# Two feed-forward entries: planned powers on GpSimd, another home for the samples' rows, smaller result tiles

## The chip, the cores and the metric

One core of a Trainium2 chip runs the whole program. The metric is the device time of one execution in microseconds (us); less is better. The engines are named as in the profile: PE (TensorE matmuls; PEld its weight loads), DVE (VectorE), ACT (ScalarE), POOL (GpSimd) and SP (SyncE, which issues all the DMAs of this kernel).

## The reference

The program is one step of a two-layer decoder trunk, for 1024 prompt tokens and 64 sample tokens (8 sequences of 8), width 1024, all in float32. Layer 0 mixes tokens with a gated MLP (gMLP), layer 1 with sliding-window attention. After either mixer comes the same pair of norms and then a SwiGLU feed-forward part. The change sits around the second and third line of this loop body:

```python
out = mixer(rms_norm(x))                    # gMLP @ sg_w_out, or attention @ sw_w_o + sw_b_o
x = x + rms_norm(out, norm_post[layer])
h = rms_norm(x, f_norm_pre[layer])
x = x + rms_norm((silu(h @ w_gate) * (h @ w_up)) @ w_down, f_norm_post[layer])
```

where `rms_norm(x, g) = x * rsqrt(mean(x*x) + 1e-6) * g`.

## The kernel before

Every float32 operand of a matmul is held as a high and a low half, and a product is three matmuls. The high half is an ACT copy, the low half a DVE subtraction.

The kernel runs through these stages: gMLP mixer, its projection (`project`), the entry into the first feed-forward part, the two feed-forward products, the exit, then keys, values, queries and attention, the second projection with a bias, the second entry and the second feed-forward part. The tokens are nine blocks: blocks 0 to 7 are 128 prompt rows each, block 8 (`NB`) the 64 sample rows. In the projection's second half the blocks come in the order 0 to 6, 8, 7.

**The entry** is what this case is about. For each block, PE runs a chain of 24 matmuls (block 8: 16) into a PSUM bank. Then ACT squares it with a row sum (L1005), DVE multiplies by the norm's weight (L1009), DVE makes the mean (L938) and POOL raises it to a power (L939), DVE adds the scaled result to the residual rows in two instructions (L1014) and SP stores them (L1015). ACT squares the sum (L1036), DVE and POOL make mean and power again (L938, L939; the samples' rows are 64 high), and ACT makes the normalised copy h (L1039). The residual rows come by DMA (L995) into a ring of 3 tiles named `rows`.

The feed-forward product uses a scheme with fewer products: seven operand forms, x1, x2 and y2, taken from the h blocks directly, and t1 to t4, differences of them (DVE, L1081, 128x512 each). The form t2 of pair i needs h of the blocks i and i+4, so the last ones need blocks 7 and 3. Each form is turned by PE transposes into one of three PSUM banks `aux` (L1051; the samples' turn is L1101), and each bank is then copied to a high half by ACT (L1055) and a low half by DVE (L1059). PE multiplies by the weights meanwhile (`part`, L1271 to L1273). Weights of the feed-forward part arrive by DMA in `raw` tiles (L416), ACT scales them (L424, four instructions) and makes the high half (L1611, or L340 elsewhere), DVE the low half (L1615, L341) and the sums of two weights (L360 to L363).

**What sets the order.** For PE, ACT and DVE in the entry, `Plan` writes the order when the program is built. It is a list scheduler: each task has an engine, a cost from the table `TIME`, the tasks it waits for, and resources that it takes and gives back (`act` and `tmp` tiles, the `rows` ring, PSUM banks `bank` and `aux`). Mean and power are one task on DVE, with the power's time as a delay behind it. The order on each engine is then kept as written: an instruction whose input is late holds up all that stand behind it. Elsewhere a scheduler of the compiler sets the order, from due times that the kernel gives it.

**Tiles of the mixers' results.** `rows` of the projection are 16 `act` tiles in the class whose methods are `at` and `pieces`: one tile for each of 8 features and each half of 512 tokens. They are given back eight at a time, behind the chains of blocks 3 and 7.

**The bias rows** of the second projection (`ones2`, `ones8` and `both`) are made at the head of `project`: POOL memsets and casts (L1137 to L1144), a DMA of `in_sw_b_o`, and a split. Each chain of the second projection ends in one matmul with them (L1154).

## Time and profile before

| what | us |
|---|---|
| median of 3 runs | 2172.33 (2169.41 to 2173.25) |
| the profiled execution, its own time | 2174.07 |
| its span, first to last instruction | 2172.3 |
| PE busy | 2122.9 (98%) |
| DVE, ACT, POOL busy | 1360.2 (63%), 1041.2 (48%), 191.0 (9%) |

The profile is of one execution. The entry of layer 0 lies at about 303 to 376 us, the attention stage at about 1083 to 1345 us, the second projection from 1345 us and the second entry's end at about 1475 us. Beside busy time the trace gives the clock that TensorE was granted: 1.00 is 2.4 GHz, 0.50 is 1.2 GHz.

### The profile page before, as it was taken

Reading aid. Unit: us, or ns where it says so; the run is one execution under the profiler, and the core shown is the slowest. Engines: PE = TensorE matmul, PEld = TensorE weight load, DVE = VectorE, ACT = ScalarE, POOL = GpSimd, SP = SyncE. Lnnn points to the kernel's source line nnn. Section 1 sums busy time; section 2 is a strip of 40 time slices with the busy share of each in tenths; the row PEclk is TensorE's granted clock in tenths of the full one; section 3 lists DMA queues with packets and bytes.
Section 4 is the critical chain, followed back from the end, with each engine's and each line's share of the span. In section 5 each row is a group of like instructions: output and inputs, shape, how many; then the busy total and the mean of one; then the engine's idle time right before and its main releaser. Section 6 shows DMA issues by size and latency. Waiting matters only on the chain.

```text
span 2172.3 us, 29400 instructions
## 1 busy us (share of the span) xinstructions
PE 2122.9 (98%) x11088; PEld 1817.3 (84%) x11088; DVE 1360.2 (63%) x2147; ACT 1041.2 (48%) x2083; POOL 191.0 (9%) x226
## 2 busy tenths in 40 slices
PE   8999998999999999999899999999999999999998
PEld 7999987788888888888698887878888888888886
DVE  5455557656665666566757767467656666665676
ACT  5234555444444443434657655365444454434342
POOL 1322301000000000000402222020000000000001
PEclk9999999999999999999899998999999999999999
DMA  4210332232232328756432111241232232268574
GB/s 146 67 39 30 97 111 93 69 99 90 94 101 87 105 97 300 243 189 215 154 87 52 48 35 55 79 145 55 95 98 95 100 97 79 95 229 289 174 255 148
DMA packets 175492, 257.11 MB, mean 118 GB/s; under 512 B 24515, under 2 KB 104629, under 8 KB 175350
## 3 DMA queue, kind: packets, MB, share of 16 engines
q1 hardware_dynamic: 175350, 255.24, 36.0%
q8 instruction: 87, 1.43, 0.3%
q14 instruction: 55, 0.45, 0.1%
HBM read 188.96 MB, written 60.62 MB: 115 GB/s over the span
## 4 chain that ended last, share of the span: by engine, by line
PE 90%; DVE 5%; DMA 2%; ACT 2%; issue 1%; POOL 1%; SPq 0%; POOLq 0%; DVEq 0%; ACTq 0%
PE bank L1497 14%; PE bank L1271 12%; PE bank L1272 12%; PE bank L1273 12%; PE bank L580 5%; PE bank L581 5%; PE bank L582 4%; PE aux L1497 4%; PE bank L957 2%; PE bank L958 2%; PE bank L959 2%; PE bank L1351 2%; PE bank L1350 2%; PE aux L1505 2%; PE aux L1051 1%; PE aux L878 1%
## 5 line engine op out<-in xcount | busy, mean ns | idle before, releaser
L1271 PE MATMUL bank<-act,act 128*128 128x512 f32 x1232 | 486.5, 395 | 4.1 <-DVE tmp L1405 4.1
L1272 PE MATMUL bank<-act,act 128*128 128x512 f32 x1232 | 483.9, 393 | 2.3 <-DVE act L1059 2.3
L1273 PE MATMUL bank<-act,act 128*128 128x512 f32 x1232 | 481.0, 391 | 0.0
L1497 PE MATMUL bank<-act,act 128*128 128x512 f32 x1452 | 341.7, 389 | 0.0
L341 DVE TENSOR_TENSOR act<-raw,act 128x1024 fp32r<-128x1024 f32 x201 | 245.6, 1223 | 126.6 <-ACT act L340 118.8
L1497 PEld LDWEIGHTS bank<-act,act 128*128 128x128 f32 x1452 | 272.4, 188 | 56.5
L340 ACT ACTIVATE act<-raw 128x1024 fp32r<-128x1024 f32 x201 | 212.4, 1059 | 214.8 <-PE bank L1351 73.7
L1271 PEld LDWEIGHTS bank<-act,act 128*128 128x128 f32 x1232 | 232.7, 189 | 50.3 <-DVE tmp L1405 5.0
L1273 PEld LDWEIGHTS bank<-act,act 128*128 128x128 f32 x1232 | 232.3, 189 | 49.4
L1272 PEld LDWEIGHTS bank<-act,act 128*128 128x128 f32 x1232 | 232.7, 189 | 46.3 <-DVE act L1059 2.8
L586 ACT ACTIVATE act<-act 128x1024 fp32r<-128x1024 f32 (+5 forms) x194 | 166.0, 904 | 186.7 <-PE bank L1497 66.7
L587 DVE TENSOR_TENSOR act<-act,act 128x1024 fp32r<-128x1024 f32 (+5 forms) x194 | 194.2, 1042 | 57.0 <-ACT act L586 43.3
L580 PE MATMUL bank<-act,act 128*128 128x384 f32 (+1 forms) x624 | 207.4, 334 | 3.9 <-ACT act L586 2.1
L582 PE MATMUL bank<-act,act 128*128 128x384 f32 (+1 forms) x624 | 207.0, 333 | 0.4 <-DVE act L341 0.4
L581 PE MATMUL bank<-act,act 128*128 128x384 f32 (+1 forms) x624 | 206.9, 332 | 0.0
L939 POOL TENSOR_TENSOR tok<-tok,expo 128x1 f32<-128x1 f32 (+1 forms) x63 | 61.9, 992 | 1573.3 <-DVE tok L938 1573.2
L424 ACT ACTIVATE raw<-raw,vcol 128x256 f32<-128x256 f32 x352 | 152.1, 498 | 76.7 <-DMA raw<-in_f_w_up 43.9
L580 PEld LDWEIGHTS bank<-act,act 128*128 128x128 f32 x624 | 118.0, 190 | 6.7 <-ACT act L586 2.5
L582 PEld LDWEIGHTS bank<-act,act 128*128 128x128 f32 x624 | 118.2, 190 | 1.6 <-issue 0.9
L581 PEld LDWEIGHTS bank<-act,act 128*128 128x128 f32 x624 | 118.4, 190 | 1.0 <-issue 0.9
L957 PE MATMUL bank<-act,act 128*128 128x512 f32 x256 | 101.5, 399 | 0.9 <-DVE tok L984 0.6
L958 PE MATMUL bank<-act,act 128*128 128x512 f32 x256 | 100.3, 392 | 0.0
(277 smaller groups left out, 3127.7 us busy)
## 6 DMA issues: line engine op xcount, KB each, us to landing
act<-in_f_w_down SPq DMA_DIRECT2D x90, 512.0 KB
raw<-in_f_w_gate SPq DMA_DIRECT2D x44, 512.0 KB
raw<-in_f_w_up SPq DMA_DIRECT2D x44, 512.0 KB
act<-hid_s SPq DMA_DIRECT2D x40, 512.0 KB
rows<-stream SPq DMA_DIRECT2D x24, 512.0 KB
hid_x<-rows SPq DMA_DIRECT2D x44, 256.0 KB
hid_s<-act SPq DMA_DIRECT2D x44, 256.0 KB
hid_s<-rows SPq DMA_DIRECT2D x44, 256.0 KB
```

Source lines behind the costliest of these rows:

```text
L340: nc.scalar.activation(self.hi, raw, AF.Copy)
L341: nc.vector.tensor_tensor(self.lo, raw, self.hi.bitcast(F32), op=ALU.subtract)
L424: nc.scalar.activation(v, v, AF.Copy, scale=col("f_norm_pre", e.gain[1] + j, e.gain[0]))
L580: nc.tensor.matmul(out[:, :n], h, xh[:, cs:cs + n], start=begin, stop=False)
L581: nc.tensor.matmul(out[:, :n], h, xl[:, cs:cs + n], start=False, stop=False)
L582: nc.tensor.matmul(out[:, :n], l, xh[:, cs:cs + n], start=False, stop=end)
L586: nc.scalar.activation(hi, src, AF.Copy)
L587: nc.vector.tensor_tensor(lo, src, hi.bitcast(F32), op=ALU.subtract)
L1271: nc.tensor.matmul(ps, h, xh, start=begin and k == 0, stop=False, skip_group_check=not begin)
L1272: nc.tensor.matmul(ps, h, xl, start=False, stop=False, skip_group_check=not begin)
L1273: nc.tensor.matmul(ps, l, xh, start=False, stop=k == 3, skip_group_check=not begin)
L1497: nc.tensor.matmul(ps, x, w, start=begin and e == k == 0, stop=end and e == n - 1 and k == 2, skip_group_check=adds)
```

## The change

1. Mean and power become two tasks. `mean` stays on DVE; `root` is a task on POOL, whose order is now the plan's too, with a cost of 600 instead of 950. A new resource `port`, of which there is one, is held from the mean to the end of the add (first power), or from the mean to a new one-column DVE copy `seen` (second power), which reads the power's result. The form differences, the weights' sums and low halves take the same resource. So the plan puts none of these on DVE while a power is in flight.
2. The samples' residual rows are fetched into an `act` tile of their own, outside the ring of three, and one block earlier.
3. A tile of the mixers' results now holds two features by 256 tokens instead of one feature by 512; four tiles come back after each of blocks 1, 3, 5 and 7. Writes that cross a multiple of 256 tokens are cut in two: 13 more instructions on ACT and 13 more on DVE.
4. The bias rows are made at step 2 of the attention stage instead of in `project`.
5. The silu of product 2 waits for the h copies of all blocks.

```diff
+    def root(b, j):
+        m = tokens(b)
+        nc.gpsimd.tensor_tensor(tok[:m, j + 1, b:b + 1], tok[:m, j, b:b + 1], expo[:m, :1], op=ALU.pow)
...
-            self.r[b] = special([P, D], "rows", bufs=ROWS)
+            self.r[b] = act_tile()[:, :D] if own else special([P, D], "rows", bufs=ROWS)
...
-            i1 = plan.add("DVE", TIME["col"], lambda: inverse(b, 3, tok[:m, 2, b:b + 1], tok[:m, 1, b:b + 1]), [sq])
-            ad = plan.add("DVE", TIME["add"], add, [(i1, TIME["pow"]), ti, fetched],
-                          give={"tmp": 1, **({"act": 1} if b % 2 or b == NB else {})})
+            port = {"port": 1}
+            i1 = plan.add("DVE", TIME["col"], lambda: mean(b, 3, tok[:m, 2, b:b + 1], tok[:m, 1, b:b + 1]), [sq], take=port)
+            r1 = plan.add("POOL", TIME["pow"], lambda: root(b, 3), [i1], give=port)
+            ad = plan.add("DVE", TIME["add"], add, [r1, ti, fetched], take=port,
+                          give={"tmp": 1, "port": 1, **({"act": 1} if b % 2 or b == NB else {})})
...
+            i2 = plan.add("DVE", TIME["col"], lambda: mean(b, 6, tok[:m, 5, b:b + 1], EPS), [s2], take=port)
+            r2 = plan.add("POOL", TIME["pow"], lambda: root(b, 6), [i2])
+            plan.add("DVE", TIME["col"], lambda: nc.vector.tensor_copy(seen[:m, b:b + 1], tok[:m, 7, b:b + 1]), [r2],
+                     give=port)
...
-                d2 = plan.add("DVE", TIME["tt"], lambda f=diff: f("t2"), [d1], take={"tmp": 1})
+                d2 = plan.add("DVE", TIME["tt"], lambda f=diff: f("t2"), [d1], take={"tmp": 1, "port": 1}, give=port)
...
-                m = min(t0 + n, (e // HN + 1) * HN) - e
+                m = min(t0 + n, (e // (2 * P) + 1) * 2 * P) - e
...
+            if b == NB:
+                fetched = plan.add(None, TIME["dma"], lambda: ent.fetch(NB, True), [at[(i + 1) % 2]], take={"act": 1})
...
-                    give["act"] = {3: 8, 7: 8, NB: 1 + (bias is not None)}.get(b, 0)
+                    give["act"] = {1: 4, 3: 4, 5: 4, 7: 4, NB: 1 + (bias is not None)}.get(b, 0)
...
-                                  [(t, TIME["pe"]), ev2.get(0)], take={"rows": 2} if q == 0 else {}, give={"bank": 1})
+                                  [(t, TIME["pe"]), ev2.get(0)] + ent.ends, take={"rows": 2} if q == 0 else {}, give={"bank": 1})
...
+        if st == BIAS:
+            bias = bias_rows("sw_b_o")
```

Line numbers move by 1 to 21: the mean is L939 after the change, the power L944, the fetch L1004, the add L1023, the second square L1046, the `seen` copy L1051, the h copy L1053, the turns L1067, their high halves L1071, the differences L1097, the scale L426, the weights' halves L1632 and L1636.

On DVE, near the end of the second entry, the order before has the differences close behind the mean of the last prompt block (128 high) and of the samples (64 high), while POOL still raises those means to their power:

```order
L1081 TENSOR_TENSOR act_12602<-act_12805,act_12602 128x512
L938 TENSOR_SCALAR tok_69<-tok_69 128x1
L1081 TENSOR_TENSOR act_12698<-act_12886,act_12698 128x512
L1081 TENSOR_TENSOR act_12709<-act_12912,act_12709 128x512
L1081 TENSOR_TENSOR tmp_13059<-act_12805,act_12602 128x512
L1081 TENSOR_TENSOR tmp_13064<-act_12886,act_12698 128x512
L1081 TENSOR_TENSOR act_12716<-act_12990,act_12716 128x512
```

After the change a `seen` copy stands behind each of these means:

```order
L1097 TENSOR_TENSOR act_12769<-act_12957,act_12769 128x512
L1097 TENSOR_TENSOR tmp_13089<-act_12823,act_12638 128x512
L1097 TENSOR_TENSOR tmp_13094<-act_12866,act_12682 128x512
L939 TENSOR_SCALAR tok_69<-tok_69 128x1
L1051 COPY seen_70<-tok_69 128x1
L1097 TENSOR_TENSOR tmp_13108<-act_12957,act_12769 128x512
L939 TENSOR_SCALAR tok_69<-tok_69 64x1
L1051 COPY seen_70<-tok_69 64x1
L1097 TENSOR_TENSOR act_12776<-act_13052,act_12776 128x512
```

The last pair's difference (into act_12776) still comes last of its kind, but three of the others now stand ahead of the mean that its h copy needs, and none between that mean and its power.

On ACT, at the end of the first entry, the h copies before stand with the silu's table load between the last prompt block's copy and the samples':

```order
L1039 ACTIVATE act_3349<-rows_3206,tok_69 128x1024
L1036 ACTIVATE act_3310,tok_69<-rows_3351 64x1024
L1682 ACT_TABLE_LOAD
L1682 ACTIVATE rows_3441<-bank_3345 128x512
L1039 ACTIVATE act_3310<-rows_3351,tok_69 64x1024
L1055 ACTIVATE act_3474<-aux_3455 128x512
```

After the change the samples (64 high, now read from an `act` tile) are ahead of the last prompt block, and the silu comes behind both:

```order
L1046 ACTIVATE act_3356,tok_69<-act_3280 64x1024
L1691 ACTIVATE tmp_3442<-bank_3416 128x512
L1046 ACTIVATE act_3399,tok_69<-rows_3300 128x1024
L1053 ACTIVATE act_3356<-act_3280,tok_69 64x1024
L1053 ACTIVATE act_3399<-rows_3300,tok_69 128x1024
L1703 ACT_TABLE_LOAD
L1703 ACTIVATE rows_3481<-bank_3393 128x512
L1125 ACTIVATE act_3499<-aux_3471 128x8x64
```

The copies of the turned forms (act_3474 before, the samples' act_3499 after) stand directly behind the samples' h copy before, and behind the silu after.

Also on ACT, some 30 us earlier in the first entry, block 3's h copy before stands behind one scale of weights, `raw_3106`, with the next one, `raw_3138`, behind it:

```order
L424 ACTIVATE raw_3106<-raw_3106,vcol_103 128x256 x4
L1039 ACTIVATE act_3103<-rows_3043,tok_69 128x1024
L1611 ACTIVATE act_3178<-raw_3106 128x1024
L1036 ACTIVATE act_3150,tok_69<-rows_3066 128x1024
L424 ACTIVATE raw_3138<-raw_3138,vcol_103 128x256 x4
L1055 ACTIVATE act_3198<-aux_3184 128x512
```

After the change both scales (`raw_3058`, not shown, and `raw_3132`) and the square of block 4 stand ahead of it:

```order
L426 ACTIVATE raw_3132<-raw_3132,vcol_104 128x256 x4
L1014 ACTIVATE act_3181,tok_69<-bank_3120 128x512
L1053 ACTIVATE act_3129<-rows_3073,tok_69 128x1024
L1071 ACTIVATE act_3215<-aux_3207 128x512
L1014 ACTIVATE act_3222,tok_69<-bank_3167 128x512
```

The first turn of x1, whose copy is act_3198 before and act_3215 after, needs this h copy. It stands at the same place in PE's order in both kernels, within the chain of block 5.

## Rows read from the trace of the kernel before

**Rows 1.** Page, part 1: busy time, share, instructions of each engine.

```profile
PE 2122.9 (98%) x11088; PEld 1817.3 (84%) x11088; DVE 1360.2 (63%) x2147; ACT 1041.2 (48%) x2083; POOL 191.0 (9%) x226
```

**Rows 2.** PE's waits, whole span: engine, line, releaser: total, times, longest.

```profile
PE aux L1051 <- DVE act L1059: 4.9, 2, 4.7
...
PE bank L1271 <- DVE tmp L1405: 4.1, 2, 2.8
...
PE aux L1941 <- POOL sc L1924: 3.0, 2, 1.5
PE aux L1051 <- DVE tmp L1081: 2.8, 2, 2.6
...
PE bank L1272 <- DVE act L1059: 2.3, 1, 2.3
```

**Rows 3.** Windows: length; PE, PEld, DVE, ACT, POOL busy; PEclk, DMA share, GB/s.

```profile
365.20:371.80 6.60, 6.44 (x27) 5.18 (x28) 4.57 (x8) 2.13 (x4) 0.00 (x0) 0.50 0.00 0
...
1460.90:1471.00 10.10, 8.81 (x35) 6.85 (x36) 8.27 (x15) 5.44 (x9) 2.13 (x1) 0.50 0.01 2
```

**Rows 4.** Timeline, first entry: start, duration, engine; in brackets idle before and releaser.

```profile
349.72 0.51 SPq L995 DMA_DIRECT2D rows<-in_x_sample  x1
...
353.77 0.74 DVE L1014 SCALAR_TENSOR_TENSOR rows<-act,tok,rows 64x512 f32<-64x512 f32 x1 [3.83 <-DMA rows<-in_x_sample]
```

**Rows 5.** Timeline, end of the first entry.

```profile
359.44 2.48 DVE L1081 TENSOR_TENSOR act<-act 128x512 f32<-128x512 f32 x4
359.59 3.33 POOL L939 TENSOR_TENSOR tok<-tok,expo 64x1 f32<-64x1 f32 x1 [3.38 <-DVE tok L938]
...
362.96 1.15 ACT L1039 ACTIVATE act<-rows,tok 64x1024 f32<-64x1024 f32 x1 [2.60 <-POOL tok L939]
```

**Rows 6.** Timelines of POOL, ACT and DVE, end of the second entry.

```profile
1456.49 2.74 POOL L939 TENSOR_TENSOR tok<-tok,expo 128x1 f32<-128x1 f32 x1 [5.78 <-DVE tok L938]
...
1459.26 1.15 ACT L1039 ACTIVATE act<-rows,tok 128x1024 f32<-128x1024 f32 x1 [2.33 <-POOL tok L939]
...
1460.44 0.69 DVE L1081 TENSOR_TENSOR act<-act,act 128x512 f32<-128x512 f32 x1 [1.63 <-ACT act L1039]
```

**Rows 7.** Timelines of POOL and DVE: a power with nothing on DVE beside it.

```profile
319.89 0.55 POOL L939 TENSOR_TENSOR tok<-tok,expo 128x1 f32<-128x1 f32 x1 [1.60 <-DVE tok L938]
...
320.48 0.75 DVE L1014 SCALAR_TENSOR_TENSOR rows<-act,tok,rows 128x512 f32<-128x512 f32 x1 [0.66 <-POOL tok L939]
```

**Rows 8.** Timelines of SP, ACT and PE: weights, block 3's h copy, first turn.

```profile
319.72 0.38 SPq L416 DMA_DIRECT2D raw<-in_f_w_up  x1
...
323.05 0.38 SPq L416 DMA_DIRECT2D raw<-in_f_w_gate  x1
...
324.25 1.70 ACT L424 ACTIVATE raw<-raw,vcol 128x256 f32<-128x256 f32 x4
325.85 1.14 ACT L1039 ACTIVATE act<-rows,tok 128x1024 f32<-128x1024 f32 x1
...
330.54 1.71 ACT L424 ACTIVATE raw<-raw,vcol 128x256 f32<-128x256 f32 x4 [1.56 <-DMA raw<-in_f_w_gate]
...
326.58 0.78 PE L1051 MATMUL aux<-ident,act 128*128 128x128 f32 x4
```

**Rows 9.** Timeline of ACT, second entry: a scale behind its DMA.

```profile
1432.81 1.71 ACT L424 ACTIVATE raw<-raw,vcol 128x256 f32<-128x256 f32 x4 [1.68 <-DMA raw<-in_f_w_gate]
```

**Rows 10.** Timeline of ACT, head of the second projection.

```profile
1365.62 1.06 ACT L586 ACTIVATE act<-act 1x1024 fp32r<-1x1024 f32 x1 [5.40 <-DMA act<-in_sw_b_o]
```

**Rows 11.** Groups of POOL in attention: busy, mean ns; idle before, releasers.

```profile
L1924 POOL TENSOR_TENSOR sc<-sc,sx 128x512 f32<-128x512 f32 x34 | 36.1, 1064 | 125.2 <-DVE sx L1923 65.1 <-PE bank L581 10.6 <-ACT sc L1919 10.5
...
L1138 POOL CAST act<-act 128x1024 fp32r<-128x1024 f32 x1 | 1.0, 1037 | 0.1
```

**Rows 12.** Windows of attention and of its middle: columns as in Rows 3.

```profile
1083.00:1345.00 262.00, 253.30 (x1903) 227.62 (x1903) 175.60 (x452) 161.11 (x559) 54.47 (x61) 0.96 0.21 51
...
1266.00:1277.00 11.00, 11.00 (x63) 9.62 (x63) 2.43 (x6) 2.06 (x10) 1.04 (x1) 0.53 0.19 52
```

More of the change, by code (lines that the diff above doesn't have):

```diff
@@ L199, in trunk_kernel @@
     tok = mk(cpool, [P, 8, NB + 1], F32, "tok")
+    seen = mk(cpool, [P, NB + 1], F32, "seen")
     identr = mk(cpool, [P, P], F32R, "ident")
@@ L1081, in diff @@
                     nc.vector.tensor_tensor(t, u, w, op=ALU.subtract)
-                d1 = plan.add("DVE", TIME["tt"], lambda f=diff: f("t1"), [h[i], h[i + 4]] + x[:4])
-                d2 = plan.add("DVE", TIME["tt"], lambda f=diff: f("t2"), [d1], take={"tmp": 1})
-                d3 = plan.add("DVE", TIME["tt"], lambda f=diff: f("t3"), [d1])
-                d4 = plan.add("DVE", TIME["tt"], lambda f=diff: f("t4"), [d2] + x[4:])
+                port = {"port": 1}
+                d1 = plan.add("DVE", TIME["tt"], lambda f=diff: f("t1"), [h[i], h[i + 4]] + x[:4], take=port, give=port)
+                d2 = plan.add("DVE", TIME["tt"], lambda f=diff: f("t2"), [d1], take={"tmp": 1, "port": 1}, give=port)
+                d3 = plan.add("DVE", TIME["tt"], lambda f=diff: f("t3"), [d1], take=port, give=port)
+                d4 = plan.add("DVE", TIME["tt"], lambda f=diff: f("t4"), [d2] + x[4:], take=port, give=port)
                 for n, t in zip(("t1", "t2", "t3", "t4"), (d1, d2, d3, d4)):
@@ L1125, in operand, with bias_rows @@
             return t[:, :HN], t[:, HN:2 * HN]
+    def bias_rows(name):
+        ones2, ones8 = mk(cpool, [P, P], F32R, "ones2"), mk(cpool, [P, P], F32R, "ones8")
+        both, one, b0, b1 = act_tile(F32R)[:, :D], tmp([P, P]), act_tile()[:, :D], act_tile(F32R)[:1, :D]
+        nc.gpsimd.memset(b0, 0.0)
+        nc.gpsimd.tensor_copy(both, b0)
+        nc.gpsimd.memset(one, 0.0)
+        nc.gpsimd.memset(one[:2, :], 1.0)
+        nc.gpsimd.tensor_copy(ones2, one)
+        nc.gpsimd.memset(one[:, NS:], 0.0)
+        nc.gpsimd.tensor_copy(ones8, one)
+        b0 = b0[:1, :]
+        nc.sync.dma_start(b0, a[name])
+        split(both[:1, :], b1, b0)
+        nc.sync.dma_start(both[1:2, :].bitcast(F32), b1.bitcast(F32))
+        return both, ones2, ones8
     def project(rows, ready, res, post, bias=None, early=None):
@@ L1153, in product @@
             if bias is not None and only in (None, KD - 1):
-                nc.tensor.matmul(ps if b == NB else ps[:tokens(b), :], ones8 if b == NB else ones2, both[:, h * HN:(h + 1) * HN], start=False, stop=True)
+                nc.tensor.matmul(ps, bias[1 + (b == NB)], bias[0][:, h * HN:(h + 1) * HN], start=False, stop=True)
                 flow.pe(HN / 2.4)
@@ L1184, in step @@
             product(box.ps, b, 1, units, slots, True, k)
-        plan = ent.plan = Plan({"act": NACT - held, "tmp": NTMP, "rows": ROWS, "bank": 5, "aux": 3})
+        plan = ent.plan = Plan({"act": NACT - held, "tmp": NTMP, "rows": ROWS, "bank": 5, "aux": 3, "port": 1})
         prev, done = None, {}
@@ L1189, in project @@
         for i, b in enumerate(ORDER):
-            fetched = plan.add(None, TIME["dma"], lambda b=b: ent.fetch(b), [at[i % 2]], take={"rows": 1})
+            if b == NB:
+                fetched = plan.add(None, TIME["dma"], lambda: ent.fetch(NB, True), [at[(i + 1) % 2]], take={"act": 1})
+            else:
+                fetched = plan.add(None, TIME["dma"], lambda b=b: ent.fetch(b), [at[i % 2]], take={"rows": 1})
             for k in range(KD):
@@ L1206, in project @@
         ent.after_blocks(plan, done)
+        ent.ends = list(done.values())
         ent.prev = prev
@@ L1642, in weights @@
                             lo[q, "sums"] = plan.add("DVE", TIME["sums"], lambda q=q: W.owner[q].sums(),
-                                                     [lo[q, "b1"], lo[q, "b2"]])
+                                                     [lo[q, "b1"], lo[q, "b2"]], take={"port": 1}, give={"port": 1})
                         a0 = lo[q, "sums"]
@@ L1647, in weights @@
                     last = h
-                    lo[key] = plan.add("DVE", TIME["tt10"], lambda box=box: low(box[0]), [h])
+                    lo[key] = plan.add("DVE", TIME["tt10"], lambda box=box: low(box[0]), [h], take={"port": 1}, give={"port": 1})
             def product(q, bank_of, un, o, name, begin, extra=(), give=None):
@@ L1746, in begin @@
                 does[n]()
-            with tc.manual_schedule(engines={PE, mybir.EngineType.Activation, mybir.EngineType.DVE}):
+            with tc.manual_schedule(engines={PE, mybir.EngineType.Activation, mybir.EngineType.DVE, mybir.EngineType.Pool}):
                 plan.run()
@@ L2130, in trunk_kernel @@
     ent = project(ys, lambda b: ygate[min(b // 3, 2)].is_open, lambda b: up.out[:P if b < NB else NS, b, :],
-                  ("sw_norm_post", 0), bias="sw_b_o", early=early)
+                  ("sw_norm_post", 0), bias=bias, early=early)
     ffn(1, ent, True)
```

51 lines of the change are left out of this document (19 added, 32 removed).

## The prediction
> **What bounds the kernel now.** I read the page first: PE is busy for 2122.9 us of a span of 2172.3 [rows 1]. So about 49 us are PE's idle time, and the rest is matmul work that this change leaves as it is, except for its order. Next come PE's waits over the whole span, because only what ends one of them can shorten the run [rows 2]. Three belong to the stages that the change rewrites: 4.7 us on turns (PE transposes) that wait for low halves (L1051 <- L1059), 2.3 us on products that wait for a low half (L1272 <- L1059), both in the first entry, and 2.6 us on turns that wait for the differences (L1051 <- L1081) in the second. Third, the windows around them: behind the first entry's waits PE ran at 0.50, its 1.2 GHz level, for at least 6.6 us, behind the second entry's for 10.1 us [rows 3]. Work done at 0.50 takes twice as long, so half of each window is lost: 3.3 and 5.05 us. What the change can give back is thus 7.0 + 3.3 = 10.3 us in the first entry and 2.6 + 5.05 = 7.65 us in the second, 17.95 us in all.
>
> Last, the timelines, for what made these waits.
> - The 2.3 us: the samples' rows were asked for at 349.72, behind the stores on SP's queue. DVE had the add of the samples next and stood idle for 3.83 us until they landed [rows 4]. The low halves queued behind that add are what PE waited for.
> - The 4.7 us: the samples' second power took 3.33 us, beside four differences on DVE that lasted 2.48 us together. ACT stood for 2.60 us with the samples' h copy next in its order; the high halves of the turned forms are behind it [rows 5]. So `aux` banks stayed full, and PE could not turn.
> - The second entry: the power of block 7 took 2.74 us beside differences, its h copy then came at 1459.26, and the difference that needs it at 1460.44 [rows 6].
> - A power with nothing beside it on DVE took 0.55 us [rows 7]. That is the whole case for the resource `port`: 3.33 and 2.74 against 0.55.
>
> **The change part by part.**
>
> *Powers and the port.* With no difference beside a power, the samples' h copy comes 3.33 - 0.55 = 2.8 us earlier and block 7's 2.2 us earlier. The other part of these waits was order: in the first entry a table load and a silu stood ahead of the samples' copy on ACT, in the second six differences stood ahead of the one that PE wanted. In the new order the silu stands behind both h copies, and three differences stand ahead of block 7's mean. Following the durations of the trace along the new order, the last t2 difference of the first entry ends about 10.8 us after the end of block 7's chain, and PE has about 11.5 us of products and turns in hand; in the second it is 8.5 against 10.2 us. So I take both waits as gone, with 0.7 and 1.7 us to spare: a thin cover. Each us by which a difference comes later than that is a us of PE, with up to 3.3 us more if the clock falls again as in [rows 3].
>
> The price is paid on DVE. It stood idle for 0.66 us between a mean and the op that needed its power [rows 7]; the `seen` copy makes it do so at each of the 18 second powers, 18 x 0.66 = 11.9 us at most, where the plan puts nothing else between. DVE is idle for a third of the span, and the low halves that wait behind a `seen` delay PE only near the end of each entry: there, two such stalls, 1.3 us, are within the times just given.
>
> *The samples' rows.* Asked for one block (24 matmuls) earlier and outside the ring, they land before the add: the 3.83 us idle time of DVE goes, and with it the 2.3 us of PE. The store moves past nothing that PE waits for.
>
> *What the new order puts late.* On ACT, block 3's h copy, which ran at 325.85 and ended 0.4 us after PE began the turns that need it (326.58, PE did not wait) [rows 8], now stands behind one more scale of weights. That scale's transfer took 330.54 - 323.05 = 7.5 us from issue; the one before it 324.25 - 319.72 = 4.5 us [rows 8]. The low half that frees its tile now stands ahead of block 3's add on DVE, which I put at 3.4 us earlier, so issue at 319.65. Then the scale starts between 324.2 and 327.2, and with 1.71 for it, 0.6 for block 4's square and 1.14 for the copy, h is there between 327.6 and 330.6, while PE wants it at about 326.9. So PE waits 0.7 to 3.7 us; I take 2.2, the middle, since the two transfers are equally near. In the second entry the like scale waited 1.68 us for its DMA [rows 9] and the two scales ahead of block 3's copy leave a wait between 0 and 2.6; I take 1.3. If such a wait lowers the clock, each costs another 1.7 to 3.4 us; I count 1.3 for the two together, since waits as short as 2.3 us were not followed by a fall at once, and the one of 2.6 was.
>
> *Smaller result tiles.* 13 more instructions on ACT and on DVE, of about 0.43 us (a scale's quarter, 128x256, is 1.71 / 4 [rows 8]), so 5.6 us on each, spread over two mixers where both have slack; on the path I count nothing, and up to 1 us if the pieces before PE's next chain are the ones that are cut. What they free earlier, four tiles instead of eight, lets turns be planned sooner; that is in the order already.
>
> *Bias rows.* ACT waited 5.40 us for `in_sw_b_o` at the head of the second projection [rows 10], with PE busy meanwhile: 0, at most a gain of 0.6 us. The casts go to POOL in early attention, about 1.04 us each [rows 11], where POOL multiplies between DVE and PE, and PE has waited 3.0 us in all for it [rows 2]: from 0 to 3 us.
>
> *Attention.* The order there is rewritten by the compiler's scheduler, since tiles and due times moved. It has 262.0 - 253.30 = 8.7 us of idle PE and a mean clock of 0.96, that is some 10 us [rows 12]. A new order can move either way; I take 0, with 5 us to both sides. The 2.8 us wait behind the weights' sums (L1271 <- L1405) [rows 2] has the same order around it and stays.
>
> *The sum.* First entry -10.3 + 2.2 = -8.1; second -7.65 + 1.3 = -6.35; clock after the new waits +1.3; together -13.2. Against the profiled execution's own 2174.07 this gives 2160.9. That execution lay 1.7 us above the median of 2172.33, so against the median it is 2159.1. I say 2160.
>
> **The rivals.**
>
> *The dips of the clock stay.* In the middle of attention the clock was 0.53 over 11 us in which PE was busy throughout [rows 12]. So it can fall without a visible wait, where PE works in small pieces, and the turns at the entry's end are small pieces too. Then 3.3 + 5.05 us don't come back and no further 1.3 is lost: -7.0 - 2.6 + 2.2 + 1.3 = -6.1, 2168.0, or 2166.2 by the median. Against it: the two windows of [rows 3] follow directly behind the waits of 4.7 and 2.6 us. The Trainium skill speaks for this rival ("TensorE: Matmul & The Clock Gate", section "A second HAM failure mode: psum-queue depth-cycling"): it tells of a kernel whose clock goes up and down because PE idles very briefly between groups of matmuls as it cycles through PSUM banks, without one long wait. By that rule the sum would be the 2168.0 just given; the attention window agrees with it, the entry's windows don't need it.
>
> *One wait for another.* The h copy of block 3 takes the place of the waits removed: 3.7 and 2.6 us, and the clock falls behind both, 3.4 us each. Net -17.95 + 6.3 + 6.8 = -4.85: 2169.2, or 2167.5. For it: the 0.4 us by which that copy was in time before. Against it: the weights' DMA is asked for earlier.
>
> *Slower, by attention.* More result tiles are open at a time (pairs by two blocks: up to eight where there were six), and the bias tile is held through the stage. If `act` tiles run out there, the query copies and the weights' splits wait for each other, and PE with them, at each of the four pairs. Were the stage's 8.7 us of waits and 10 us of half clock to double, it would cost 18.7 us, more than the 13.2 gained: about 2179.6, or 2178. It decides from 13.2 us up. Against it: PE's waits there now go to POOL and DVE results, none to a tile's release.
>
> *The port doesn't do what it says.* If the powers stay long for another reason, only the 2.3 us of the samples' rows are gained and the new waits are paid: -2.3 + 3.5 = +1.2, so 2173.5 by the median. Against it: 0.55 against 3.33, with the differences the only other work on DVE.
>
> *More than that.* Attention's order turns out better by 5 us and the new waits don't come: -17.95 - 5 = -23, about 2150.
>
> **How the numbers follow.** Forecast 0.50, dips stay 0.12, one wait for another 0.14, slower by attention 0.11, port without effect 0.07, more 0.06. The range reaches from the best case, 2150, to just above the port without effect, 2173; about 2 in 10 is outside, mostly the slower case. A change of 0.2%, 4.3 us, is about what a measurement of this kernel can tell from none: faster is below 2168.0. Forecast, more, and three quarters of the first two rivals lie there, less a little for attention's spread: 0.74. The port without effect and the rest of the two: 0.14. Slower: 0.12.
>
> **What would show it.** In the profile after: no power of the entries above 1 us; no PE wait on L1067 for L1075 or L1097 over 1 us at the two entries' ends; no stretch at 0.50 right behind them; DVE no longer idle for the samples' rows; ACT's scales L426 ahead of block 3's h copy and a PE wait of about 2 us at the first turn of x1; attention within 5 us of 262.0. I am wrong if powers stay at 2 to 3 us, if the first turns wait for over 4 us, or if attention grows by more than 10 us.

## The result, and the profile after

The changed kernel takes 2151.76 us (median of 5 runs, 2150.56 to 2152.42), the kernel before 2173.25 in the same session (5 runs, 2169.41 to 2175.41). The ratio is 0.9901, with a 95% interval of 0.9887 to 0.9916: faster by 21.5 us, where 12.3 was forecast (2160 against the 2172.33 known then). The time lies inside the range, near its lower end of 2150; the direction is right, and the gain is 1.75 times the forecast. Most of what follows is about the part that was not forecast.

The page after the change, part 1, and then PE's waits within the two entries (242 to 385 us, and 1345 to 1470 us), engine, line and releaser with total, times and longest:

```profile
PE 2114.1 (98%) x11088; PEld 1811.2 (84%) x11088; DVE 1366.3 (64%) x2178; ACT 1042.7 (48%) x2096; POOL 182.0 (8%) x226
```

```profile
PE aux L1067 <- DVE act L1075: 0.4, 1, 0.4
...
PE aux L1067 <- DVE act L1075: 0.3, 1, 0.3
```

These two rows are all that is left of the 7.0 and 2.6 us of [rows 2]. The same instructions as in [rows 5] and [rows 6], POOL's powers at the ends of the two entries:

```profile
354.10 0.53 POOL L944 TENSOR_TENSOR tok<-tok,expo 64x1 f32<-64x1 f32 x1 [3.04 <-DVE tok L939]
355.67 0.55 POOL L944 TENSOR_TENSOR tok<-tok,expo 128x1 f32<-128x1 f32 x1 [1.04 <-DVE tok L939]
...
1439.57 0.55 POOL L944 TENSOR_TENSOR tok<-tok,expo 128x1 f32<-128x1 f32 x1 [3.84 <-DVE tok L939]
1441.04 0.54 POOL L944 TENSOR_TENSOR tok<-tok,expo 64x1 f32<-64x1 f32 x1 [0.92 <-DVE tok L939]
```

0.53 to 0.55 us, where 3.33 and 2.74 stood. Not all powers of the entries are that short. Three lie above 1 us, all early in an entry and all first powers: 1.48 us at 311.74 in the first entry, 1.63 and 1.47 us at 1391.55 and 1395.43 in the second. Beside each runs the low half of a weight on DVE:

```profile
311.58 1.21 DVE L1636 TENSOR_TENSOR act<-raw,act 128x1024 fp32r<-128x1024 f32 x1
313.25 0.75 DVE L1023 SCALAR_TENSOR_TENSOR rows<-act,tok,rows 128x512 f32<-128x512 f32 x1 [0.46 <-POOL tok L944]
...
311.74 1.48 POOL L944 TENSOR_TENSOR tok<-tok,expo 128x1 f32<-128x1 f32 x1 [2.83 <-DVE tok L939]
```

The first part of the change says that the port is held from the mean to the end of the add. The code does not do that: `r1` gives it back at the power's planned end and the add takes it anew, and no `seen` copy follows a first power. So a low half may be planned between the two, and DVE then runs it at once, beside the power. Each time DVE then stood for about 0.46 us; PE did not wait there.

And the ends of the entries in windows (columns as in [rows 3]), where stretches at 0.50 stood:

```profile
350.00:386.00 36.00, 35.57 (x219) 30.71 (x218) 27.10 (x49) 23.22 (x41) 2.06 (x3) 1.00 0.10 32
1440.00:1471.00 31.00, 30.72 (x198) 26.67 (x197) 24.36 (x44) 19.62 (x34) 0.66 (x2) 1.00 0.04 12
```

PE is busy throughout at the full clock, so neither the waits nor the half clock came back.

To see where the 21.6 us between the two spans (2172.3 and 2150.7) went, I cut each trace at five moments of PE that every variant has: the first chain matmul of the first projection, the last turn of the first entry, the longest gap of the exit, the last chain matmul of the second projection, and the last turn of the second entry. The lengths between them, in us, for both kernels and all the experiments below:

```
                 up to     first     to the  exit to      second   rest
                 first     chain to  exit    last chain   entry's  to the
                 chain     last turn         (attention)  end      end
before           240.5     149.9     677.1   378.9        43.3     682.6
after            242.0     141.2     676.1   373.4        35.3     682.7
noport           239.9     150.9     674.6   374.7        37.1     682.5
oldpow           240.1     146.1     674.7   375.0        37.1     682.5
portonly         240.8     145.5     674.5   377.9        36.3     682.6
noseen           242.0     144.6     676.6   371.9        34.9     682.4
oldrows          241.6     141.4     676.4   373.4        35.6     683.7
rowsonly         240.8     142.2     675.0   378.2        39.2     682.4
oldtiles         241.7     144.6     676.7   371.6        38.4     682.6
oldbias          239.9     141.5     674.4   376.8        35.2     682.7
biasonly         241.3     148.2     676.5   375.8        44.3     682.4
oldsilu          244.2     143.6     674.9   374.6        35.6     682.9
siluonly         241.6     150.1     674.8   377.9        43.4     682.3
probe            242.7     142.1     676.5   374.9        35.2     683.0
```

The second column is called the first entry below, the fourth the stretch with attention. From before to after: the first entry -8.7, the second entry's end -8.0, the stretch with attention -5.5, the feed-forward part behind the first entry -1.0, and 1.5 later at the start, which no part of the change touches: over all the traces it lies between 239.9 and 244.2. The sum is -21.7 against -21.6 measured. Windows of 0 to 50 us, columns as in [rows 3], show the start's 1.5 us as clock, 1.00 in the kernel before and 0.97 in the changed one:

```profile
0.00:50.00 50.00, 40.80 (x222) 35.36 (x223) 26.95 (x55) 28.35 (x60) 5.77 (x19) 1.00 0.47 146
...
0.00:50.00 50.00, 40.53 (x210) 35.44 (x211) 26.76 (x55) 27.55 (x58) 5.05 (x18) 0.97 0.45 146
```

### The profile page after: what moved, and what is told of

Read it like the earlier page. It is cut to its first block, busy times and chain, and to the rows that moved or that the text cites. A ratio compares the mean times of both kernels' runs of the same rounds, so it can differ in the third digit from the quotient of the medians.

```text
span 2150.7 us, 29463 instructions
## 1 busy us (share of the span) xinstructions
PE 2114.1 (98%) x11088; PEld 1811.2 (84%) x11088; DVE 1366.3 (64%) x2178; ACT 1042.7 (48%) x2096; POOL 182.0 (8%) x226
## 4 chain that ended last, share of the span: by engine, by line
PE 91%; DVE 4%; ACT 2%; DMA 1%; issue 1%; POOL 0%; SPq 0%; POOLq 0%; ACTq 0%
PE bank L1518 14%; PE bank L1292 13%; PE bank L1293 12%; PE bank L1294 12%; PE bank L582 5%; PE bank L584 5%; PE bank L583 5%; PE aux L1518 4%; PE bank L966 2%; PE bank L968 2%; PE bank L967 2%; PE bank L1372 2%; PE bank L1371 2%; PE aux L1526 2%; PE aux L1067 1%; PE aux L2085 1%
## 5 line engine op out<-in xcount | busy, mean ns | idle before, releaser
L588 ACT ACTIVATE act<-act 128x1024 fp32r<-128x1024 f32 (+3 forms) x199 | 166.6, 886 | 181.5 <-PE bank L1518 68.0
L589 DVE TENSOR_TENSOR act<-act,act 128x1024 fp32r<-128x1024 f32 (+3 forms) x199 | 193.9, 1016 | 47.1 <-ACT act L588 36.2
L944 POOL TENSOR_TENSOR tok<-tok,expo 128x1 f32<-128x1 f32 (+1 forms) x63 | 56.3, 900 | 1565.4 <-DVE tok L939 1565.4
L426 ACT ACTIVATE raw<-raw,vcol 128x256 f32<-128x256 f32 x352 | 152.0, 498 | 74.6 <-DMA raw<-in_f_w_up 44.1
```

The costliest lines, as they stand in the source:

```text
L426: nc.scalar.activation(v, v, AF.Copy, scale=col("f_norm_pre", e.gain[1] + j, e.gain[0]))
L588: nc.scalar.activation(hi, src, AF.Copy)
L589: nc.vector.tensor_tensor(lo, src, hi.bitcast(F32), op=ALU.subtract)
```

## The experiments

The first theory: powers that run beside DVE's differences make the h copies late; the port takes that away, and the rest of the change matters little. The rivals are the other parts: the samples' tile, the result tiles, the silu's place, the bias rows. So each part was taken out of the changed kernel, and all but the tiles were put alone into the kernel before; the tiles alone were not tried. Times are medians; the ratio behind each is to the kernel before in the same session (the changed kernel's is 0.9901, with 0.9887 to 0.9916). The traces are of one execution each.

**Does DVE hold POOL up, and with which instructions?** The cost in dispute, measured by itself (`probe`).

```diff
+            def last_mean():
+                mean(b, 6, tok[:m, 5, b:b + 1], EPS)
+                w0, w1, pr = self.post[:m, :HN], self.post[:m, HN:], self.h[b][:m, :HN]
+                if b == 0:
+                    nc.vector.tensor_tensor(pr, w0, w1, op=ALU.subtract)
+                elif b == 2:
+                    nc.vector.tensor_scalar(pr, w0, 1.0, 0.0, op0=ALU.mult, op1=ALU.add)
+                elif b == 3:
+                    nc.vector.tensor_copy(pr, w0)
+                elif b == 4:
+                    nc.vector.tensor_tensor(pr, w0, w1, op=ALU.subtract)
+                    nc.vector.tensor_tensor(pr, w0, w1, op=ALU.subtract)
...
+            i2 = plan.add("DVE", TIME["col"], last_mean, [s2], take=port)
```

> The changed kernel with extra DVE instructions right behind the second means of four blocks, on 128x512 floats in SBUF, while POOL raises the mean to its power (they write a tile whose content is not used yet): block 0 one subtraction of two SBUF inputs, block 2 a tensor_scalar of one input, block 3 a copy of one input, block 4 two subtractions. If only two SBUF inputs hold POOL up: powers of about 1.2 us in block 0 and 1.9 in block 4, 0.55 in blocks 2 and 3. If any DVE work in SBUF does: blocks 2 and 3 also 0.9 to 1.2. If nothing on DVE does and the long powers had another cause: 0.55 in all.

The timelines of DVE and of POOL at the four places of the first entry, and at one more where DVE reads PSUM (start, duration, engine, line):

```profile
316.02 0.68 DVE L1052 TENSOR_TENSOR act<-act 128x512 f32<-128x512 f32 x1
...
316.18 0.93 POOL L944 TENSOR_TENSOR tok<-tok,expo 128x1 f32<-128x1 f32 x1 [2.19 <-DVE tok L939]
...
322.65 0.42 DVE L1054 TENSOR_SCALAR act<-act 128x512 f32<-128x512 f32 x1
...
322.82 0.66 POOL L944 TENSOR_TENSOR tok<-tok,expo 128x1 f32<-128x1 f32 x1 [0.26 <-DVE tok L939]
...
326.72 0.42 DVE L1056 COPY act<-act 128x512 f32<-128x512 f32 x1
...
326.88 0.66 POOL L944 TENSOR_TENSOR tok<-tok,expo 128x1 f32<-128x1 f32 x1 [3.41 <-DVE tok L939]
...
338.66 0.68 DVE L1058 TENSOR_TENSOR act<-act 128x512 f32<-128x512 f32 x1
339.37 0.69 DVE L1059 TENSOR_TENSOR act<-act 128x512 f32<-128x512 f32 x1
...
338.82 0.93 POOL L944 TENSOR_TENSOR tok<-tok,expo 128x1 f32<-128x1 f32 x1 [4.59 <-DVE tok L939]
...
333.52 0.68 DVE L1018 TENSOR_TENSOR tmp<-bank,act 128x512 f32<-128x512 f32 x1
...
333.68 0.55 POOL L944 TENSOR_TENSOR tok<-tok,expo 128x1 f32<-128x1 f32 x1 [2.57 <-DVE tok L939]
```

Read the ends. The subtraction ended at 316.70, the power at 317.11; the tensor_scalar at 323.07, the power at 323.48; the copy at 327.14, the power at 327.54. Each time the power ended 0.40 to 0.41 us behind the DVE instruction, so all three hold POOL until they are over, those with one input too; they only last 0.42 us instead of 0.68. None of the three expectations had this: I had let one input either do nothing or do it as long as two. Beside DVE work that reads PSUM the power took its 0.55. And of two subtractions only the first counted (339.34 + 0.41 = 339.75 = 338.82 + 0.93): here 0.03 us lay between the two on DVE, and the power got through. In the kernel before, four differences and a fifth followed one another with no space between; the fifth ended at 362.52 and the power of [rows 5] at 359.59 + 3.33 = 362.92, again 0.40 behind. (The prediction spoke of four.) In the second entry of this run the four powers took the same 0.93, 0.66, 0.66 and 0.93 us. The low half beside a power in the changed kernel fits too: it ended at 311.58 + 1.21 = 312.79, the power at 313.22, 0.43 behind.

**The port taken away** (`noport`), with the tasks and the `seen` copies kept:

```diff
-        plan = ent.plan = Plan({"act": NACT - held, "tmp": NTMP, "rows": ROWS, "bank": 5, "aux": 3, "port": 1})
+        plan = ent.plan = Plan({"act": NACT - held, "tmp": NTMP, "rows": ROWS, "bank": 5, "aux": 3, "port": 9})
```

> The changed kernel with nine units of the resource port instead of one, so the plan may again put differences, sums and low halves on DVE beside a power; mean, power and the seen copy stay separate tasks. If it is the port that freed the two entries: powers of 2 to 4 us at both ends of the entries again, h copies late by 2 to 3 us, PE waits of 2 to 5 us with a stretch at half clock behind, so 2158 to 2168 us against 2151.8. If the order alone (samples ahead of block 7, silu last) did it: powers long again in places but no PE wait, 2150 to 2154 us.

2163.78 us, ratio 0.9967 (0.9956 to 0.9978): 0.0066 of the 0.0099 gained are gone, some 14 us. That the port matters is what the first theory said; the way it does so is only in part the one of that theory. The power at the first entry's end, and PE's waits in 300 to 400 us:

```profile
361.38 3.33 POOL L944 TENSOR_TENSOR tok<-tok,expo 64x1 f32<-64x1 f32 x1 [2.99 <-DVE tok L939]
```

```profile
PE aux L1067 <- ACT act L1053: 4.0, 1, 4.0
PE aux L1067 <- DVE act L1075: 3.3, 1, 3.3
```

The power took 3.33 us once more, with a wait of 3.3 us behind it. But the larger wait, 4.0 us, is another: the first turns of x1, which wait for block 3's h copy. The prediction had named a wait at these turns, behind the DMA of weights. Here the copy waited for its power instead, whose mean came late on DVE (one line each of DVE, POOL and ACT):

```profile
328.57 0.69 DVE L365 TENSOR_TENSOR raw<-raw,raw 128x512 f32<-128x512 f32 x1
329.18 0.27 DVE L939 TENSOR_SCALAR tok<-tok 128x1 f32<-128x1 f32 x2
...
329.41 1.07 POOL L944 TENSOR_TENSOR tok<-tok,expo 128x1 f32<-128x1 f32 x2 [5.58 <-DVE tok L939]
...
329.99 1.15 ACT L1053 ACTIVATE act<-rows,tok 128x1024 f32<-128x1024 f32 x1 [1.70 <-POOL tok L944]
```

In this run a low half of weights stands ahead of block 3's add on DVE, and the four sums of weights (L362 to L365, 326.40 to 329.26 us) ahead of its mean. All of these take the port. In the changed kernel block 3's mean ran at 325.39 and the sums began behind it, at 328.37. So the resource does two things: it shortens powers, and it keeps the weights' work on DVE behind block 3.

**The old powers in the changed kernel** (`oldpow`): mean and power one task on DVE, no port, no `seen`.

> The changed kernel without its first part: mean and power one task with the old cost, no port, no seen copy; the samples' tile, result tiles, bias rows and silu as changed. If the port carries the entries: powers of 2 to 4 us and waits at both entries as before, only attention's 5 to 6 us gained, 2163 to 2168 us. If the other parts carry them: 2152 to 2158 us.

2158.09 us, 0.9940 (0.9922 to 0.9957). A miss for the first theory, which wanted 2163 or more. At the first entry's end there is no wait at all, though nothing keeps differences and powers apart by rule: the longest power there is 1.31 us. What is left is the first turns' wait, for the same reason as in `noport` (four sums of weights ahead of block 3's mean, which ran at 329.47):

```profile
PE aux L1061 <- ACT act L1047: 4.1, 1, 4.1
```

In the second entry a power of 2.80 us and a PE wait of 2.0 stay.

**The first part alone** (`portonly`): the other four parts taken out of the changed kernel.

> The kernel before with the first part alone: mean, power and seen copy as tasks of their own, with the port; rows ring, result tiles, bias rows and silu as before. If the port is the cause at the two entries' ends: no power over 1.5 us there, most of the 12 us between the two kernels' entries gained, attention as before: 2155 to 2163 us where the kernel before takes 2171. If the port needs the smaller result tiles, which let the turns of x1 come in time: a PE wait of 2 to 4 us at the first turns of x1, 2160 to 2168.

2161.6 us, 0.9955 (0.9939 to 0.9971). No power over 1.01 us, the second entry's end 36.3 us; and a wait of 2.6 us at the first turns, as the second expectation said. Both hold in part: the port alone nearly frees both ends (waits there of at most 0.9 us), and the first turns come late without the smaller tiles, here behind the DMA of weights that the prediction named.

**Without the `seen` copies** (`noseen`): the power's task gives the port back.

```diff
-            r2 = plan.add("POOL", TIME["pow"], lambda: root(b, 6), [i2])
-            plan.add("DVE", TIME["col"], lambda: nc.vector.tensor_copy(seen[:m, b:b + 1], tok[:m, 7, b:b + 1]), [r2],
-                     give=port)
+            r2 = plan.add("POOL", TIME["pow"], lambda: root(b, 6), [i2], give=port)
```

> The changed kernel without the seen copies: the plan still gives the port back only at a power's planned end, but DVE does not wait for it. If the copies are what makes the plan hold on the chip: some powers of 1 to 3 us again where DVE runs ahead of the plan, 2152 to 2160 us. If the planned order is enough: powers below 1.5 us, DVE spared about 10 us of waits, 2148 to 2152 us.

2153.31 us, 0.9920 (0.9905 to 0.9936), which overlaps with the changed kernel's interval. The samples' second power took 2.18 us at the first entry's end, against 0.53 in the changed kernel, so DVE does run ahead of the plan; PE waited 1.9 us for h copies at the first turns and 0.7 us at the samples' turn. The copies are what makes the plan hold, and that is worth about 3 us in the first entry (144.6 against 141.2) and nothing in the second.

**The samples' rows**, back in the ring (`oldrows`):

```diff
-            if b == NB:
-                fetched = plan.add(None, TIME["dma"], lambda: ent.fetch(NB, True), [at[(i + 1) % 2]], take={"act": 1})
...
+            fetched = plan.add(None, TIME["dma"], lambda b=b: ent.fetch(b), [at[i % 2]], take={"rows": 1})
```

> The changed kernel with the samples' residual rows back in the ring of three. If the samples' own tile is what took away the 2.3 us at the first entry: DVE idle for 2 to 4 us on those rows again, a PE wait of 1 to 3 us, 2153 to 2158 us. If the port's order alone carries the entries: 2151 to 2153 us, no PE wait.

2153.35 us, 0.9914 (0.9893 to 0.9936): no difference to the changed kernel, stage by stage (141.4 and 35.6 us). DVE doesn't wait for those rows; in the order that the port makes they are asked for at 340.62, not at 349.72 as in [rows 4].

And the same part alone in the kernel before (`rowsonly`):

> The kernel before with one part alone: the samples' residual rows in a tile of their own, asked for earlier. If the late rows are the cause of the 2.3 us wait: DVE no longer idle for them and that wait gone, the 4.7 us stay or shift, 2166 to 2169 us. If the store queue or the order is what matters: 2170 to 2173 us.

2161.77 us, 0.9954 (0.9941 to 0.9968), better than both expectations. DVE's wait for the rows is gone, and with it most of the loss at the first entry: 142.2 us against 149.9. A power of 2.13 us is still there for the samples, but it now comes early enough. PE's waits in 300 to 400 us:

```profile
PE aux L1061 <- DVE act L1069: 1.3, 1, 1.3
PE aux L1111 <- DVE act L1069: 0.8, 1, 0.8
PE aux L1061 <- ACT act L1047: 0.2, 1, 0.2
```

So the two waits of [rows 2] in the first entry were not two costs with a cause each. The reading that fits: DVE's idle time for the rows pushed all the work behind it, the samples' power among it, against the moment when PE needed it. The new order on DVE also leaves three differences beside that power instead of five, and the run does not part the two.

In the second entry, where the prediction did not look for it, DVE waited for the samples' rows too. With their own tile that wait is gone and the end of the entry takes 39.2 us instead of 43.3, while the power of block 7 takes the same 2.74 us as in [rows 6] (kernel before, then `rowsonly`):

```profile
1454.34 0.75 DVE L1014 SCALAR_TENSOR_TENSOR rows<-act,tok,rows 64x512 f32<-64x512 f32 x1 [2.30 <-DMA rows<-stream]
...
1444.31 2.74 POOL L944 TENSOR_TENSOR tok<-tok,expo 128x1 f32<-128x1 f32 x1 [4.06 <-DVE tok L939]
```

PE's wait of 2.6 us for the differences is gone, but three others, of 1.3, 1.3 and 0.8 us, stand there: PE idles 3.4 us in this stage instead of 3.2. The 4.1 us are clock, since no stretch at half clock follows.

**The silu's place**, alone in the kernel before (`siluonly`) and free again in the changed kernel (`oldsilu`, whose edit is shown; the other is its reverse):

```diff
-                                  [(t, TIME["pe"]), ev2.get(0)] + ent.ends, take={"rows": 2} if q == 0 else {}, give={"bank": 1})
+                                  [(t, TIME["pe"]), ev2.get(0)], take={"rows": 2} if q == 0 else {}, give={"bank": 1})
```

> The kernel before with one part alone: the silu of product 2 behind all h copies. Its order on DVE at the first entry's end is that of the kernel before, so the samples' power still runs beside four differences. If the power is the cause of the 4.7 us wait: power of about 3.3 us and wait of 4 to 5 us stay, 2170 to 2173 us. If the table load and silu ahead of the samples' copy are: the wait shrinks by about 1.9 us and more with the clock, 2164 to 2168 us.

> The changed kernel with the silu of product 2 free again to go ahead of the last h copies. If its place matters at the entries' ends even with the port: a PE wait of 1 to 2 us there and up to 3.4 us of clock, 2153 to 2157 us. If not: 2151 to 2153 us.

Alone: 2172.15 us, 1.0003 (0.9993 to 1.0013). The power took 3.33 us and PE waited:

```profile
PE aux L1061 <- DVE act L1069: 4.7, 1, 4.7
PE bank L1286 <- DVE act L1069: 2.3, 1, 2.3
```

Both are to the digit those of [rows 2]. So the silu's place alone gives nothing there. In the kernel before, table load and silu ran while ACT could not go on anyway; the power was what held the copy. Taken out of the changed kernel: 2155.44 us, 0.9922 (0.9904 to 0.9940), with PE waits of 1.1, 1.1 and 0.5 us in the first entry (143.6 against 141.2) and 0.6 us in the second: small, and the intervals of the two ratios overlap.

**The result tiles** as before (`oldtiles`):

```diff
-                i, o = divmod(t0, 2 * P)
...
+                h, o = divmod(t0, HN)
...
-                    give["act"] = {1: 4, 3: 4, 5: 4, 7: 4, NB: 1 + (bias is not None)}.get(b, 0)
+                    give["act"] = {3: 8, 7: 8, NB: 1 + (bias is not None)}.get(b, 0)
```

> The changed kernel with the mixers' results again in one tile for each feature and half of the tokens, given back eight at a time. The change gained about 5.7 us between the exit and the end of the second projection's chains, which no term of the prediction held. If the tiles' layout reordered attention for the better: those 5.7 us are lost, 2156 to 2159 us. If it is the bias rows' place: 2151 to 2153 us in attention, and at the entries a first turn of x1 that comes later, 0 to 3 us.

2160.95 us, 0.9951 (0.9933 to 0.9968); the traced execution, 2157.33, was the shortest of five, so the stages hold only about 5 us of the loss. It is not in attention, which is no longer than after (371.6 us), but in the entries: 144.6 and 38.4. ACT at the first turns, and what PE waited for:

```profile
328.54 1.71 ACT L426 ACTIVATE raw<-raw,vcol 128x256 f32<-128x256 f32 x4 [3.33 <-DMA raw<-in_f_w_up]
330.15 1.14 ACT L1053 ACTIVATE act<-rows,tok 128x1024 f32<-128x1024 f32 x1
```

```profile
PE aux L1067 <- ACT act L1053: 2.4, 1, 2.4
```

That is the chain that the prediction feared: weights by DMA, scale, h copy of block 3, first turn. It is real, and in the first entry the smaller tiles are what keeps it away. At the second entry's end PE waited 1.0, 0.9 and 0.4 us for DVE; what the tiles have to do with those was not settled.

**The bias rows**, back at the head of the projection (`oldbias`) and alone at the early place (`biasonly`):

```diff
+        if bias is not None:
+            bias = bias_rows(bias)
...
-        if st == BIAS:
-            bias = bias_rows("sw_b_o")
```

> The changed kernel with the bias rows made at the head of the second projection as before. If their place is what made attention shorter: 5 to 7 us longer there, 2156 to 2159 us. If it is the tiles' layout: 0 to 1 us longer, 2152 to 2153 us, with ACT waiting about 5 us for the bias DMA and PE for almost nothing.

> The kernel before with one part alone: the bias rows made at step 2 of attention. If their place made the stretch from the exit to the end of the second projection's chains shorter: 3 to 6 us off the 378.9 us that it takes in the kernel before, 2165 to 2169 us in all. If it was chance of the compiler's order in all parts together: between 375 and 384 us there, 2167 to 2176.

Back: 2157.21 us, 0.9941 (0.9916 to 0.9966); attention 376.8 us against 373.4, the entries unchanged. The five executions lie between 2152.31 and 2161.56, and the traced one is the shortest: it started 2.1 us sooner and was 1.7 us shorter between the first entry and the exit, which hides the 3.4 us. What the longer executions lost is not seen. Alone: 2168.44 us, 0.9989 (0.9980 to 0.9998); attention 375.8 against 378.9. Over all fourteen traces the stretch takes 371.6 to 375.8 us in the nine with the rows made early and 376.8 to 378.9 in the five without, and PE's waits between 1085 and 1420 us add up to 5.2 to 6.2 us in the nine and 8.2 to 9.8 in the five. All of PE's idle time in the stretch shows the same: 13.7 to 15.5 us in the nine, 17.2 to 19.9 in the five. So the place of the bias rows is worth about 3 us, as PE's idle time. The clock makes up most of the rest: it stood at 0.50 for 40.9 us of the stretch before and 34.1 after, and half of the difference is 3.4 us; but over the traces this goes up and down with either place (31 to 44 us), so no part of the change is shown to have caused it. In `oldbias` one part of how can be read:

```profile
PE bank L1174 <- DMA act<-act: 1.6, 1, 1.6
...
PE bank L966 <- DVE tok L993: 0.6, 1, 0.6
```

L1174 is the bias matmul; it waited for the DMA that brings the low half of the bias into its row. In the kernel before that matmul did not wait. There, and in the three others that keep the old place beside `oldbias`, PE stands twice between about 1181 and 1194 us, for 0.9 to 1.5 us each; no kernel with the early rows has more than one wait of 0.6 us there. Why the compiler's order differs at that point was not settled.

## Why the prediction was right, and where it was off

*The sum.* It had -13.2; the stages give -21.7. The 8.5 us between them are attention 5.5, the entries 2.25 (-16.7 where -8.1 and -6.35 stood), no loss of clock behind new waits 1.3, the feed-forward part 1.0, less the 1.5 of the start. The time is inside the range because its lower end was set by the rival "more than that".

*The mechanism of the powers.* Right: 0.53 to 0.55 us at the entries' ends, and `probe` shows the cause by itself. Off in two details: an instruction with one input holds POOL as well, for its shorter time; and the sign "no power of the entries above 1 us" failed for three first powers (1.47 to 1.63 us), since the port does not guard them on the chip. The step from power to wait is borne out at the second entry's end: PE idled 2.0 to 4.3 us there in the six kernels whose power of block 7 took 2.74 to 2.80 us, and 0.0 to 1.2 us in seven of the eight others (2.4 in `oldtiles`, with a power of 2.06 us). In the first entry it is only part of the cause: `rowsonly` leaves 1.3 of the 4.7 us with a power of 2.13 us, and in `oldpow` the order of the other parts leaves powers of at most 1.31 us and no wait at that end.

*The waits at the entries' ends.* Right that both go with their clock: -8.7 and -8.0 us, where the sum had -8.1 and -6.35. The nearness of the first pair is partly luck: the waits and the half clock of [rows 2] and [rows 3] would give -10.3 + 0.4 = -9.9, so 1.2 us came short, and the 2.2 us counted for a new wait did not come. Why 1.2 came short is not resolved, since the order of products and turns around the last turn also differs. At the second end PE's idle time fell from 3.2 to 0.3 us and the clock gave back 5.1, together the 8.0.

*The samples' rows.* Their own tile takes away the 3.83 us of DVE and the 2.3 us of PE. It does so alone too, and more than that: 7.7 us of the first entry and, by the clock alone, 4.1 at the second's end, where the prediction had not seen DVE's 2.30 us. But with the port it is worth nothing (`oldrows`). The prediction costed each part against the kernel before as if the gains added up. Alone, port and rows gain 4.4 and 7.7 us in the first entry, 7.0 and 4.1 at the second's end; together with the rest 8.7 and 8.0.

*What the new order puts late.* The terms +2.2, +1.3 and +1.3 for new waits and their clock were mis-sized: all three are 0 (the 0.4 and 0.3 us that PE still waits stand at the entries' ends). The chain named is real, as `oldtiles` (2.4 us) and `portonly` (2.6) show, the two with the port and the old tiles; `noport` (4.0) and `oldpow` (4.1) wait at the same turns behind another chain, the weights' sums on DVE. In the changed kernel the weights came 5.2 us after issue, within the 4.5 to 7.5 of the bounds, and PE came to these turns at 328.73 instead of 326.58:

```profile
328.73 0.90 PE L1067 MATMUL aux<-ident,act 128*128 128x128 f32 x4
```

ACT's copy of block 3 ended at 329.25, 0.5 us into these turns, of which only the fourth reads block 3. Of PE's 2.15 us, 1.5 are the later start of this run. A run that starts early need not wait much more: `oldbias`, which has the same entry and started 2.1 us sooner, had its weights sooner as well and PE waited 0.4 us.

*Smaller tiles.* Counted at nothing on the path; they are worth 3.4 us in the first entry, mostly by keeping that chain in time, and 3.1 at the second's end. The prediction mentioned that four tiles come back earlier and put it aside as part of the order.

*Bias rows and attention.* The term that was off most. It took 0, at most 0.6 us, from the rows at the projection's head, because PE was busy while ACT waited 5.40 us for the DMA [rows 10], and 0 for attention's new order. Measured: about 3 us for the place, 5.5 in all. The casts cost nothing on POOL: PE's wait for it in attention fell from 3.0 to 0.4 us. That nobody waited for ACT in one trace did not mean that nothing hung on the place of this work.

*The wait behind the weights' sums* was put down as unchanged; its longest fell from 2.8 to 1.8 us, and the stretch from the first entry to the exit by 1.0. No run tells which part did that.

*The rivals.* "The dips of the clock stay" fell: no stretch at 0.50 is left at either entry's end, so these followed the waits. "One wait for another" is what happens in `portonly` and `oldtiles`, and by another chain in `noport` and `oldpow`; "slower, by attention" and "the port doesn't do what it says" have nothing for them. "More than that", 2150 us with a chance of 0.06, is where the time came out, by the way it named: attention better by 5 us and the new waits absent.

## What to carry to other kernels

A part that is worth nothing when taken out may be worth most of the gain when put in alone, and the other way round: where several edits work on one late chain, cost the chain, not the edits. In these runs a small instruction on GpSimd beside VectorE work in SBUF ended only when that work had a gap, so plan the two as one resource, and make the plan hold with a real wait. And when work that "hides" at a stage's head moves away, look for what the wait for it, or its place in the compiler's order, kept back.

## What the hardware showed unexpectedly

- A power on POOL (128x1) ended 0.40 to 0.41 us after the DVE instruction beside it, for two SBUF inputs (0.68 us long) as for one (0.42 us), in float32 on 128x512; with one input in PSUM it kept its 0.55 us. 0.03 us between two DVE instructions was enough for POOL to get through (0.93 us, also beside the sums L362 and L363 of the changed kernel); behind five without a gap it took 3.33 us. Beside one subtraction of 128x1024 (1.21 to 1.23 us) it took 1.47 to 1.63.
- In the kernel before, one PE wait of 2.6 us was followed by 10.1 us at half clock [rows 3]; in `noport` and `oldpow` waits of 4.0 and 4.1 us went with 3.4 us, in `oldtiles` and `portonly` waits of 2.4 and 2.6 us with none. The same wait differs too: the 4.7 us of the first entry went with 6.8 us at half clock in the kernel before and with 3.4 in `biasonly`. What a wait costs in clock is thus not in proportion to its length.
